# A 90-degree rotation of 96 planes: the first store waits for the loads, and the group of four slabs goes fourth

## The chip, the core and the metric

The kernel runs on one core of one Trainium2 chip. The metric is the device time in microseconds (us). Before the change it is 123.41 us, the median of three runs (123.36 to 123.59).

## The reference

The input `x` has 32 x 3 planes of 256 x 256 float32 numbers, 25.17 MB. Each plane is turned by 90 degrees clockwise; nothing is calculated.

```python
def reference(x):
    return np.rot90(x, k=-1, axes=(-2, -1)).astype(np.float32)
```

Every byte must be read once and written once, so 50.33 MB pass through the DMA engines.

## The kernel before

**Tiling.** The input is seen as 24,576 rows of 256 numbers and cut into 12 slabs of 2,048 rows (2 MB each): a slab is 128 partitions x 16 rows, 16 KB in each partition. All 12 slabs fit on the chip at once. They are held in five groups, given by `sizes` (line 38): 2, 2, 4, 2, 2 slabs. Each group has one tile `u0` to `u4` (line 41), and nothing in it is used twice: data come in, are turned in place, and go out from the same tile. Small side buffers hold what an in-place turn would overwrite: `spare[0]` and `spare[1]` in PSUM (line 45) and `extra` in SBUF (line 46), each half a slab.

**Loads.** SyncE (SP) issues all DMAs. Group 0 comes in with three transfers (lines 55 and 56: 1, 1 and 2 MB). Each later group comes in with as many transfers as it has slabs, 2 MB each (line 61). A transfer takes every I-th partition (`[i::I]`, with I the slabs of the group) and two runs `a` in each. That makes 13 loads. Loads have no wait of their own except that the program has eight semaphores for landings, used in turn: a transfer's issue waits until the transfer eight places ahead has landed.

**Turning.** VectorE (DVE) does the turning by 32 x 32 transposes of a quarter of two slabs at a time, 128 x 2048 numbers in one instruction, four for a group of two slabs and eight for the group of four. For groups 1 to 4 (`turn_group`, lines 77 to 95) it first transposes one quarter per pair of slabs into a side buffer (line 85), then the other three in place (line 90); then ScalarE (ACT) copies the held quarter back (line 95). Group 0 has its own form (lines 65 to 75). Line 97 says which side buffer a group uses: group 1 `extra`, group 2 both spares, group 3 `spare[0]`, group 4 `spare[1]`.

**Stores.** After all of that, in program order, stand the stores, 2 MB each: two for group 0 (line 103), then for each group two per pair of slabs (line 108), each from every second partition (`[a::2]`). That makes 12 stores. They stand behind the loads in SP's order, and each waits for its data, for its landing semaphore and for nothing else. All 25 transfers go through one hardware queue. Descriptors move 8, 16 or 32 KB at a time.

The program's order of the groups is the order of loading, of turning and of storing.

Of the kernel before, what the change touches and what calls it, by code (L numbers as in the profile page):

```python
# [1 line left out]

# [4 lines left out]


@with_exitstack  # L10
def kernel(
    ctx: ExitStack,
    tc: tile.TileContext,
    x: bass.AP,
    out: bass.AP,
):

    nc = tc.nc
    fp32 = mybir.dt.float32

    B, C, H, W = x.shape
    P = nc.NUM_PARTITIONS
    R = 16  # L30
    E = R * W
    hw = R // 2
    low, high = slice(0, hw), slice(hw, R)

    rows_in = x.rearrange("b c h w -> (b c h) w")
    rows_out = out.rearrange("b c h w -> (b c h) w")

    sizes = (2, 2, 4, 2, 2)
    first = [sum(sizes[:n]) for n in range(len(sizes))]
    groups = [  # L40
        ctx.enter_context(tc.tile_pool(name=f"group{n}", bufs=1)).tile([P, s, E], fp32, name=f"u{n}")
        for n, s in enumerate(sizes)
    ]
    psum = ctx.enter_context(tc.tile_pool(name="psum", bufs=1, space=bass.MemoryType.PSUM))
    spare = [psum.tile([P, E // 2], fp32, name=f"spare{h}") for h in range(2)]
    extra = ctx.enter_context(tc.tile_pool(name="extra", bufs=1)).tile([P, E // 2], fp32, name="extra")

    def rows_of(rows, n):
        return rows[first[n] * P * R : (first[n] + sizes[n]) * P * R]


    ld = rows_of(rows_in, 0).rearrange("(s i p r) w -> s i p (r w)", s=2, i=2, p=P)
    home = [groups[0][:, s].rearrange("p (i f) -> p i f", i=2) for s in range(2)]
    for i in range(2):
        nc.sync.dma_start(out=home[0][:, i], in_=ld[1, i])  # L55
    nc.sync.dma_start(out=home[1], in_=ld[0].transpose([1, 0, 2]))  # L56
    for n in range(1, len(sizes)):
        I = sizes[n]
        ld = rows_of(rows_in, n).rearrange("(a i m r) w -> i m a (r w)", a=2, i=I, m=P // I)
        for i in range(I):  # L60
            nc.sync.dma_start(  # L61
                out=groups[n].rearrange("p s f -> p (s f)").rearrange("p (a f) -> p a f", a=2)[i::I],
                in_=ld[i])

    def turn_slab(src, dsts):
        s = src.rearrange("p (i r g c) -> p c r g i", i=2, r=R // 2, c=R)
        for h, d in enumerate(dsts):
            d = d.rearrange("p (c k r) -> p c r k", c=hw, r=R // 2)[:, :, ::-1, ::-1]
            nc.vector.transpose(out=d, in_=s[:, h * hw : (h + 1) * hw])  # L69

    u = groups[0]
    turn_slab(u[:, 0], spare)
    turn_slab(u[:, 1], [u[:, 0, : E // 2], u[:, 0, E // 2 :]])
    for h in range(2):
        nc.scalar.copy(out=u[:, 1, h * E // 2 : (h + 1) * E // 2], in_=spare[h])  # L75

    def turn_group(n, held):
        I = sizes[n]
        T = I // 2
        K = W // (R * T)  # L80
        u = groups[n].rearrange("p s f -> p (s f)")
        src = u.rearrange("p (a t r g c) -> p t c r g a", a=2, t=T, r=R, c=R)
        dst = u.rearrange("p (i c k t r) -> p t c r k i", i=I, c=R, k=K, t=T)[:, ::-1, :, ::-1, ::-1, :]
        for t in range(T):
            nc.vector.transpose(  # L85
                out=held[t].rearrange("p (i c k r) -> p c r k i", i=I, c=hw, k=K)[:, :, ::-1, ::-1, :],
                in_=src[:, t, low, low])
        for c, r in ((low, high), (high, high), (high, low)):
            for t in range(T):
                nc.vector.transpose(out=dst[:, t, c, r], in_=src[:, t, c, r])  # L90
        back = u.rearrange("p (i c k t r) -> p t i c k r", i=I, c=R, k=K, t=T)[:, ::-1]
        for t in range(T):
            kept = held[t].rearrange("p (i c k r) -> p i c k r", i=I, c=hw, k=K)
            for i in range(I):
                nc.scalar.copy(out=back[:, t, i, low, :, high], in_=kept[:, i])  # L95

    for n, held in enumerate(([extra], spare, [spare[0]], [spare[1]]), 1):
        turn_group(n, held)


    st = rows_of(rows_out, 0).rearrange("(s i m r) w -> i m s (r w)", s=2, i=2, m=P // 2)
    for a in range(2):
        nc.sync.dma_start(out=st[a], in_=groups[0][a::2])
    for n in range(1, len(sizes)):
        st = rows_of(rows_out, n).rearrange("(a i m r) w -> a m i (r w)", a=2, i=sizes[n], m=P // 2)
        for i in range(0, sizes[n], 2):
            for a in range(2):
                nc.sync.dma_start(out=st[a][:, i : i + 2], in_=groups[n][a::2, i : i + 2])


# [1 line left out]
_INS = ['x']  # L112
_OUTS = [((32, 3, 256, 256), 'float32')]


# [23 lines left out]
```

## Time and profile before

| | us |
|---|---|
| Median of three runs | 123.41 |
| The profiled execution's own time | 123.44 |
| Its span, from the first to the last instruction | 121.6 |
| DVE busy, 24 instructions | 87.4 |
| ACT busy, 17 instructions | 14.9 |
| First transfer issued / first packet moves | 0.73 / 1.74 |
| Last of the 13 loads landed | 62.44 |
| Last of the 12 stores landed | 120.79 |

The span is the part that the trace covers; 1.8 us of the execution's time lie around it. A transfer has three times in the trace: when its instruction was issued on SP, when its packets moved on each of the 16 DMA engines, and when each engine's completion reached the semaphore; it has landed when the last of the 16 has. Rows that are marked SPq are SP's sequencer issuing DMAs. "a <- b" in the waits says that a stood idle until b was done.

### The profile page before, as it was taken

The page shows a single profiled execution, that of the slowest core. Times are in us where ns is not written, and L with a number is a line of the kernel's source. Part 1 is how long each engine was busy: PE and PEld are TensorE (multiplying, and loading weights), DVE is VectorE, ACT ScalarE, POOL GpSimd, SP SyncE. Part 2 cuts the span into 40 slices and gives each one's busy share as a digit, 9 for nine tenths or more (in the row PEclk, how much of TensorE's full clock was granted, in tenths as well). Part 3 has the DMA queues.
Part 4 walks back from the last instruction along what each step waited for, and adds up shares of the span by engine and source line. Part 5 has one row for each costly group of instructions (what it writes and reads, how often), then busy time and mean ns, then how long its engine had stood idle before and what let it go on. Part 6 is the DMA issues. An engine that isn't in the chain of part 4 may idle for free.

```text
span 121.6 us, 130 instructions
## 1 busy us (share of the span) xinstructions
DVE 87.4 (72%) x24; ACT 14.9 (12%) x17; POOL 0.2 (0%) x4
## 2 busy tenths in 40 slices
DVE  0039999999994099999999949999999995000000
ACT  0000400470004100000000354000240004100000
POOL 0000000000000000000000000000000000000000
DMA  4999999998989899999999999999999999999993
GB/s 92 423 426 434 442 431 431 436 506 356 506 356 506 350 431 431 426 431 431 377 409 431 431 431 431 442 431 431 431 431 442 431 436 431 431 431 431 431 431 135
DMA packets 3472, 50.33 MB, mean 414 GB/s; under 512 B 400, under 2 KB 400, under 8 KB 400
## 3 DMA queue, kind: packets, MB, share of 16 engines
q1 hardware_dynamic: 3472, 50.33, 97.7%
HBM read 25.17 MB, written 25.17 MB: 414 GB/s over the span
## 4 chain that ended last, share of the span: by engine, by line
DVE 42%; DMA 30%; issue 7%; SPq 4%; ACT 2%; ACTq 1%; DVEq 0%
DVE u L90 30%; DMA u<-in_x_dram 30%; DVE spare L85 12%; SPq L61 3%; ACT u L95 2%; ACTq L134 1%; SPq L55 1%; SPq L56 0%; DVEq L85 0%
## 5 line engine op out<-in xcount | busy, mean ns | idle before, releaser
L90 DVE STREAM_TRANSPOSE u<-u 128x2048 f32<-128x2048 f32 x15 | 54.7, 3665 | 0.4
L85 DVE STREAM_TRANSPOSE spare<-u 128x2048 f32<-128x2048 f32 x4 | 14.3, 3586 | 5.9 <-DMA u<-in_x_dram 4.3
L95 ACT COPY u<-spare 128x512 f32<-128x512 f32 (+1 forms) x12 | 8.0, 743 | 55.9 <-DVE u L90 55.9
L69 DVE STREAM_TRANSPOSE spare<-u 128x2048 f32<-128x2048 f32 x2 | 7.1, 3584 | 8.1 <-DMA u<-in_x_dram 8.1
L69 DVE STREAM_TRANSPOSE u<-u 128x2048 f32<-128x2048 f32 x2 | 7.8, 3990 | 0.0
L75 ACT COPY u<-spare 128x2048 f32<-128x2048 f32 x2 | 3.6, 1870 | 8.7 <-DVE u L69 8.7
L85 DVE STREAM_TRANSPOSE extra<-u 128x2048 f32<-128x2048 f32 x1 | 3.9, 3899 | 0.0
L95 ACT COPY u<-extra 128x1024 f32<-128x1024 f32 x2 | 2.0, 1043 | 11.3 <-DVE u L90 11.3
L75 ACT ACT_TABLE_LOAD x1 | 1.3, 1283 | 13.1 <-DMA u<-in_x_dram 13.1
L123 POOL MEMSET const-bfloat16-1.0<- 128x1 bf16 x1 | 0.1, 101 | 0.0
L123 POOL MEMSET const-uint8-127<- 128x1 uint8 x1 | 0.1, 101 | 0.0
L123 POOL MEMSET const-float32-0.0<- 128x1 f32 x1 | 0.1, 98 | 0.2 <-issue 0.2
L123 POOL MEMSET const-float32-1.0<- 128x1 f32 x1 | 0.1, 98 | 0.0
## 6 DMA issues: line engine op xcount, KB each, us to landing
out_dram<-u SPq DMA_DIRECT2D x12, 2048.0 KB, 20.6
u<-in_x_dram SPq DMA_DIRECT2D x11, 2048.0 KB, 32.3
u<-in_x_dram SPq DMA_DIRECT2D x2, 1024.0 KB, 5.8
```

Of the source, the lines that this page charges most:

```text
L55: nc.sync.dma_start(out=home[0][:, i], in_=ld[1, i])
L61: nc.sync.dma_start(out=groups[n].rearrange("p s f -> p (s f)").rearrange("p (a f) -> p a f", a=2)[i::I], in_=ld[i])
L69: nc.vector.transpose(out=d, in_=s[:, h * hw : (h + 1) * hw])
L75: nc.scalar.copy(out=u[:, 1, h * E // 2 : (h + 1) * E // 2], in_=spare[h])
L85: nc.vector.transpose(out=held[t].rearrange("p (i c k r) -> p c r k i", i=I, c=hw, k=K)[:, :, ::-1, ::-1, :], in_=src[:, t, low, low])
L90: nc.vector.transpose(out=dst[:, t, c, r], in_=src[:, t, c, r])
L95: nc.scalar.copy(out=back[:, t, i, low, :, high], in_=kept[:, i])
L123: nc = _bacc.Bacc("TRN2", target_bir_lowering=False, num_devices=1)
L134: with _tile.TileContext(nc) as tc:
```

## The change

The groups are now 2, 2, 2, 4, 2 slabs: the group of four is loaded, turned and stored fourth, not third. The side buffers follow: group 1 `extra`, group 2 `spare[1]`, group 3 both spares, group 4 `extra`. The last load of 2 MB is cut into two of 1 MB, the first of which is called `mark`. The first store gets a dependency on `mark`, so that it waits until that load has landed, when 1 MB of loads is still to come. The stores of a group are two transfers whatever its size, so that the group of four leaves in two of 4 MB in place of four of 2 MB. There are now 14 loads and 10 stores.

```diff
-    sizes = (2, 2, 4, 2, 2)
+    sizes = (2, 2, 2, 4, 2)
...
     for n in range(1, len(sizes)):
         I = sizes[n]
         ld = rows_of(rows_in, n).rearrange("(a i m r) w -> i m a (r w)", a=2, i=I, m=P // I)
+        to = groups[n].rearrange("p s f -> p (s f)").rearrange("p (a f) -> p a f", a=2)
         for i in range(I):
-            nc.sync.dma_start(
-                out=groups[n].rearrange("p s f -> p (s f)").rearrange("p (a f) -> p a f", a=2)[i::I],
-                in_=ld[i])
+            if (n, i) == (len(sizes) - 1, I - 1):
+                mark = nc.sync.dma_start(out=to[i::I, 0], in_=ld[i][:, 0])
+                nc.sync.dma_start(out=to[i::I, 1], in_=ld[i][:, 1])
+            else:
+                nc.sync.dma_start(out=to[i::I], in_=ld[i])
...
-    for n, held in enumerate(([extra], spare, [spare[0]], [spare[1]]), 1):
+    for n, held in enumerate(([extra], [spare[1]], spare, [extra]), 1):
         turn_group(n, held)
...
     for a in range(2):
-        nc.sync.dma_start(out=st[a], in_=groups[0][a::2])
+        put = nc.sync.dma_start(out=st[a], in_=groups[0][a::2])
+        if a == 0:
+            tc.add_manual_dep(put.ins, mark.ins.name, mybir.DependencyInfo(
+                mybir.DependencyClass.Sync, mybir.DependencyReason.SCHED_ONLY), reason="stores after loads")
     for n in range(1, len(sizes)):
         st = rows_of(rows_out, n).rearrange("(a i m r) w -> a m i (r w)", a=2, i=sizes[n], m=P // 2)
-        for i in range(0, sizes[n], 2):
-            for a in range(2):
-                nc.sync.dma_start(out=st[a][:, i : i + 2], in_=groups[n][a::2, i : i + 2])
+        for a in range(2):
+            nc.sync.dma_start(out=st[a], in_=groups[n][a::2])
```

## The prediction

> **What bounds the kernel now.** I read the page first, its busy shares and its slices.
>
> ```profile
> DVE 87.4 (72%) x24; ACT 14.9 (12%) x17; POOL 0.2 (0%) x4
> ...
> DMA  4999999998989899999999999999999999999993
> GB/s 92 423 426 434 442 431 431 436 506 356 506 356 506 350 431 431 426 431 431 377 409 431 431 431 431 442 431 431 431 431 442 431 436 431 431 431 431 431 431 135
> ...
> q1 hardware_dynamic: 3472, 50.33, 97.7%
> ```
>
> DVE, the busiest engine, works 87.4 us of 121.6; the DMA engines are taken for 97.7%. The rate is near 431 GB/s whether they load (left half) or store (right half); the 506/356 pattern is 32 KB packets counted where they start. So the DMA queue is the bound, and only its idle or slow stretches can be won. Second, the stretches:
>
> ```profile
> 0.00:1.70 1.70, 0.00 (x0) 0.00 (x0) 0.20 (x4) 1.00 0.00 0
> 1.70:59.00 57.30, 46.39 (x13) 6.91 (x5) 0.00 (x0) 1.00 1.01 425
> 59.00:62.00 3.00, 3.00 (x2) 0.00 (x0) 0.00 (x0) 1.00 0.96 339
> 62.00:119.60 57.60, 38.06 (x11) 7.96 (x12) 0.00 (x0) 1.00 1.01 431
> 119.60:121.60 2.00, 0.00 (x0) 0.00 (x0) 0.00 (x0) 1.00 0.16 66
> ```
>
> The last two columns are DMA share and GB/s. Besides the head (1.7 us) and the tail, one place is slow: 59 to 62 us, where the queue passes from loads to stores. At 431 GB/s its bytes would take 3.00 x 339 / 431 = 2.36 us, so 0.64 us is lost. The landing records say the same: loads of 2 MB with 16 KB packets land 4.89 us apart (the 10th at 47.10, 11th 52.00, 12th 56.89), the last takes 5.55 (62.44), and stores then land every 4.84 to 4.89 us. The loss is 5.55 - 4.89 = 0.66 us on the slowest DMA engine. The 16 completions of one transfer, 0.43 us apart until then, are 0.82 us apart from there to the end: half of the engines lost some 0.25 us, half 0.6. Packets that otherwise take 0.61 us take 0.7 to 1.27 from about 59.1 us on, two microseconds before the last load's packets end.
>
> Third, SP's waits, which say why stores are already queued at that time:
>
> ```profile
> SPq L108 <- DVE u L90: 52.6, 4, 28.5
> SPq L61 <- DMA u<-in_x_dram: 14.7, 4, 4.3
> SPq L103 <- DMA u<-in_x_dram: 8.3, 2, 4.2
> ```
>
> A transfer is issued when the one eight places ahead has landed, so the first stores (the 14th and 15th transfers) go out at 27.73 and 32.51, as loads 6 and 7 land, and two of group 1 at 40.06 and 42.22. They lie behind the last loads in one queue, which keeps its order: nothing is stored until the loads are through.
>
> **The change, part by part.**
>
> *The group of four goes fourth.* The same bytes are loaded: 32 KB packets (steps of 4.855 us) and 16 KB packets (4.89) change places, sum unchanged. New landings from these steps: group 2 at 32.6, group 3 at 52.0, group 4 last. DVE goes through group 0 as now (8.1 to 23.1) and group 1 (to 38.0), then group 2 at once: 3.6 + 10.9 (a group of two with its side buffer in PSUM, the timeline's rows from 72.94 to 87.51) = 14.5, to 52.6, ACT's copies to 54.5. Group 3 takes 7.1 + 21.9 = 29.0, to 81.6; its second transpose needs `spare[1]` and comes at 56.2, after ACT's copies. ACT then needs 3.1 more: 84.6. Group 4 takes 3.9 + 11.2 = 15.1 (group 1's rows), to 96.7, with copies 98.7. DVE's waits of 4.28 us (for the four slabs) and 1.63 us (for ACT) go, but what DVE gains is hidden: the queue has six 2 MB stores to do from about 61.8, to 61.8 + 6 x 4.863 = 91.0, so group 3 (84.6) comes 6.4 us early, and group 4 (98.7) is 12 us ahead of the queue's 110.4. Cost: 0. Should that cover fail, the queue would idle by whatever DVE is late; it would take 6.4 us.
>
> *The cut load and the joined stores.* 25 transfers become 24. A transfer's completion takes each engine one packet of 9 ns and a gap, about 13 ns; two 1 MB loads at the start landed 2.51 us apart, half of the next 2 MB's 4.97. So: -0.01 us. Joined stores keep 16 KB packets; their steps should be 9.7 us. A 4 MB issue on SP is not in the trace: a 2 MB one takes 0.60 to 1.35 us, so between 0.60 and 2 x 1.35 = 2.7; the queue holds over 4 us of work then, so 0 either way.
>
> The Trainium skill ("DMA: Bandwidth & Descriptors", section Bandwidth) gives transfers of 1 MB 78% of the peak; by it the two halves would cost 0.6 us more each. The two 1 MB loads in this queue show no such loss, so I leave it out.
>
> *The wait of the first store.* Behind it on SP stand only the nine other stores and the end; no engine waits for a store. What matters is whether the DMA engines run dry before its packets come. `mark` would land at 56.89 + 4 packets x 0.613 + 0.01 = 59.36 on the slowest engine, if nothing slows it. An issue follows a landing by 0.02 to 0.09 us (42.21 to 42.22; 27.64 to 27.73): 59.45. From issue to first packet, the one place with an idle queue is the program's start: issue 0.73, packet 1.74, so 1.01 us: 60.46. A store's issue takes 0.60 to 0.65 against that one's 0.37; if packets come only after it ends, 60.74. Without the slow stretch, load packets end at 61.0 on the fastest engine, 61.43 on the slowest (12th transfer's completion packets at 56.1 to 56.4, plus 4.9). So the store's packets arrive 0.3 to 1.0 us before an engine is dry. Not free is the ramp: the first 8 KB packet took 1.1 us, later ones 0.31, so 0.8 us of ramp from HBM; for a read from SBUF there is no row, between 0 and that. With all 0.8 the first store packet ends at 60.46 + 0.8 + 0.61 = 61.87, or 62.15 from 60.74; without any delay the slowest engine would end it at 61.43 + 0.61 = 62.04. So the late arrival costs 0 to 0.11 us.
>
> What it may win are the 0.66 us. I take them to come from stores standing ready behind the loads: the engines begin reading for stores while load data are still arriving, as the slow packets fit that begin 2 us before the loads end. Held, the stores arrive when at most one packet per engine is left. Bounds: nothing is won (the loss belongs to the change of direction), or all of it, 0.66. I take nearly all, since the slow packets are load packets, which no stores would stand beside before 60.46.
>
> The skill's rule against it is in the same page, section Rules for kernel authors: issue a DMA early and wait late, so that its fixed cost is hidden. Its first-byte time for queues of this kind (some 0.6 us, section Latency and other measured facts) would put the first store packets at 60.05, earlier than the row's 1.01 us does; the row is used.
>
> **Sum**, against the profiled execution (123.44; the median of the runs is 0.03 less): last load lands at 56.89 + 4.90 = 61.79, not 62.44; the stores take 58.35 - 0.03 as now; last landing 120.11 against 120.79, so -0.68; ramp +0 to +0.11. That is 122.76 to 122.87: **122.8**.
>
> **Rivals.**
>
> *The loss stays.* Turning the queue from reading HBM to writing it costs 0.66 us wherever the stores come from. For it: stores land in an even step afterwards and the loss is a single one; against: it falls on loads. Time: 123.4 less 0.03. The same number results if the dependency turns out only to order the program and the store is issued as load 7 lands, at 32.6 us.
>
> *Slower: the engines need a longer lead than they get.* The slow packets begin 2 us before the loads end, so the engines may read about that far ahead. Held stores leave the reading side without work from about 59.1 to 60.46 or 60.74: 1.36 to 1.64 us. If that lead is lost, it decides as soon as the lead needed exceeds the 0.3 to 1.0 us left. Price: where the turn's own loss stays too, up to 1.64 us, to 125.0; where some of it is covered by packets in flight, half, 0.7 us: 124.1. For it: 1.1 us for the first packet at the start. Against: that ramp was HBM's, and a stored packet is read from SBUF.
>
> **Numbers.** Held and the loss gone (122.7 to 123.1): 0.52. Loss stays or is not held (123.2 to 123.6): 0.27. Engines run dry (123.7 to 125): 0.21. The range goes from 122.5 (the bound 122.76 less 0.2 for run-to-run spread, as the three runs differ by 0.23) to 124.1, which leaves out half of the last case. 0.2%, 0.25 us, is about what a measurement of this kernel can tell from no change: faster 0.52, same 0.27, slower 0.21. The likeliest case's own range is 122.6 to 123.1.
>
> **What would show it.** The first store issued near 59.4 us and not 27.7; `mark` landed just before, the last load at 61.8; the GB/s in 59 to 62 near 425; the spread of 16 completions staying near 0.43 us; last landing near 120.1, span near 121.0. DVE ends near 96.7 with no wait over 1 us after 23 us. If the last load lands at 61.8 but the first store over 5.2 us later, the engines ran dry. If it lands at 62.4 again, the turn itself costs. The prediction is wrong in kind if group 3's stores are issued after 91.

## The result and the profile after

The changed kernel takes 122.94 us (median of six runs, 122.88 to 123.17), the kernel before, beside it, 123.58 us (123.36 to 123.62): a ratio of 0.996 (95% interval 0.9946 to 0.9973). Between the medians that is 0.64 us less, between the means 0.54. In a later series the same pair gave 123.03 against 123.36, 0.33 us less, ratio 0.9975 (0.9965 to 0.9984). The profiled execution of the changed kernel took 122.88 us, with a span of 121.09 us (before: 123.44 and 121.65).

First the page of the changed kernel, its busy times and slices:

```profile
DVE 87.4 (72%) x24; ACT 14.9 (12%) x17; POOL 0.2 (0%) x4
...
DMA  2999999999989898999999999999999999999994
GB/s 89 428 428 422 452 433 433 433 433 433 520 346 520 346 520 346 428 422 411 433 433 428 433 433 428 417 417 433 428 433 433 433 433 433 433 433 433 433 422 184
...
q1 hardware_dynamic: 3456, 50.33, 97.6%
```

DVE works as long as before. The dip in the middle of the GB/s row (377 and 409 before, at slices 20 and 21) is gone; the 520/346 pattern, the four-slab group's 32 KB packets, has moved to the right. The stretches of the changed kernel, with the same columns as those shown of before:

```profile
0.00:1.70 1.70, 0.00 (x0) 0.00 (x0) 0.20 (x4) 1.00 0.00 0
1.70:59.00 57.30, 50.69 (x14) 8.84 (x7) 0.00 (x0) 1.00 1.00 425
59.00:62.00 3.00, 2.97 (x2) 0.00 (x0) 0.00 (x0) 1.00 1.03 437
62.00:119.60 57.60, 33.71 (x10) 6.10 (x10) 0.00 (x0) 1.00 1.00 428
119.60:121.10 1.50, 0.00 (x0) 0.00 (x0) 0.00 (x0) 1.00 0.01 0
```

The third row is the gain: 437 GB/s from 59 to 62 us where 339 stood. The fourth has a small part of it given back: 428 against 431. When the stores were issued, from the timeline of SP in the changed kernel:

```profile
59.43 1.37 SPq L106 DMA_DIRECT2D out_dram<-u  x2
60.92 25.39 SPq L113 DMA_DIRECT2D out_dram<-u  x6
```

And what SP waited for there (total us, times, longest):

```profile
SPq L106 <- DMA u<-in_x_dram: 31.2, 1, 31.2
SPq L113 <- DVE u L93: 24.3, 2, 14.7
```

The first store stands 31.2 us at its wait for the load `mark` and goes out at 59.43; before, it went out at 27.73. The landing records show what came of it (last of the 16 completions of a transfer, in us):

| | before | after |
|---|---|---|
| 22 of 24 MB loaded | 56.89 | 56.82 |
| `mark` | | 59.29 |
| Last load | 62.44 | 61.74 |
| Last store | 120.79 | 120.28 |
| From last load to last store | 58.35 | 58.54 |
| Spread of the 16 completions, last load | 0.82 | 0.28 |

The last 2 MB took 4.92 us and not 5.55: 0.63 us won at the turn. Of it, 0.19 us is lost again on the way to the end, so that the last store lands 0.51 us earlier. DVE's one wait for a load in the changed kernel is the first, until 8.06 us, and it no longer waits for ACT; its last transpose ends at 95.9.

### The profile page after: what moved, and what is told of

Same layout as the page of the kernel before. It is cut to its first block, busy times and chain, and to the rows that moved or that the text cites. A ratio compares the mean times of both kernels' runs of the same rounds, so it can differ in the third digit from the quotient of the medians.

```text
span 121.1 us, 131 instructions
## 1 busy us (share of the span) xinstructions
DVE 87.4 (72%) x24; ACT 14.9 (12%) x17; POOL 0.2 (0%) x4
## 4 chain that ended last, share of the span: by engine, by line
DVE 66%; issue 6%; DMA 6%; ACT 1%; ACTq 1%; SPq 0%; DVEq 0%
DVE u L93 39%; DVE spare L88 9%; DVE extra L88 6%; DVE u L72 6%; DVE spare L72 6%; DMA u<-in_x_dram 6%; ACT u L98 1%; ACTq L139 1%; SPq L55 0%; DVEq L88 0%; DVEq L72 0%
## 5 line engine op out<-in xcount | busy, mean ns | idle before, releaser
L72 DVE STREAM_TRANSPOSE spare<-u 128x2048 f32<-128x2048 f32 x2 | 7.1, 3586 | 8.1 <-DMA u<-in_x_dram 8.1
L98 ACT COPY u<-spare 128x512 f32<-128x512 f32 (+1 forms) x10 | 6.0, 687 | 38.5 <-DVE u L93 38.5
L88 DVE STREAM_TRANSPOSE spare<-u 128x2048 f32<-128x2048 f32 x3 | 10.7, 3588 | 0.0
L88 DVE STREAM_TRANSPOSE extra<-u 128x2048 f32<-128x2048 f32 x2 | 7.8, 3896 | 0.0
L98 ACT COPY u<-extra 128x1024 f32<-128x1024 f32 x4 | 4.0, 1043 | 22.8 <-DVE u L93 22.8
```

The lines of the kernel that those rows point to most:

```text
L88: nc.vector.transpose(out=held[t].rearrange("p (i c k r) -> p c r k i", i=I, c=hw, k=K)[:, :, ::-1, ::-1, :], in_=src[:, t, low, low])
```

## The experiments

Two theories at first. **H**: stores that stand ready behind the last loads cost 0.66 us at the turn, and the hold saves it. **G**: the gain comes from the new order of the groups or the joined stores. The prediction's slower rival, that the engines need a longer lead of store packets than 1 MB gives, is tested beside them. The lead is the time from the moment when the first store's packets could start to the end of the load packets. Each run was timed beside the kernel before on its own chip; that kernel's medians were 123.34 to 123.54 us there, its single runs 123.04 to 123.93. Of each kernel's runs a single one, the profiled execution, has a trace. Of each edit the lines that matter are shown, with ... for others, against the changed kernel unless said otherwise.

### The hold alone, and the rest alone

The kernel before with the cut load and the held store (its order and its 2 MB stores kept), shown against the kernel before:

```diff
+            if (n, i) == (len(sizes) - 1, I - 1):
+                mark = nc.sync.dma_start(out=to[i::I, 0], in_=ld[i][:, 0])
+                nc.sync.dma_start(out=to[i::I, 1], in_=ld[i][:, 1])
...
+            tc.add_manual_dep(put.ins, mark.ins.name, mybir.DependencyInfo(
...
```

> The order of the groups (2, 2, 4, 2, 2) and the 2 MB stores of the kernel before; only the cut last load and the held first store are taken from the change. Theory H (stores standing ready behind the last loads cost 0.66 us, and holding them back saves it): the last two loads land 2.45 us apart, the last near 61.8 us, the 16 completions stay about 0.3 to 0.4 us apart, and the time is 122.9 us (122.75 to 123.1). Theory G (the gain is the new order or the joined stores): the last load lands near 62.4 and the time is 123.4 to 123.6. Third possibility: less than 122.75, if the joined 4 MB stores of the change cost something.

Measured: 123.25 us, ratio 0.9989 (0.9977 to 1.0). The time lies between the two theories' ranges. The turn itself went as H says: the last load landed at 61.84, 4.90 us after the load of 22 MB, and the row of its stretches is as in the changed kernel:

```profile
59.00:62.00 3.00, 3.00 (x2) 0.00 (x0) 0.00 (x0) 1.00 1.03 437
```

The changed kernel without hold and cut:

```diff
-                mark = nc.sync.dma_start(out=to[i::I, 0], in_=ld[i][:, 0])
-                nc.sync.dma_start(out=to[i::I, 1], in_=ld[i][:, 1])
+                nc.sync.dma_start(out=to[i::I], in_=ld[i])
...
-        put = nc.sync.dma_start(out=st[a], in_=groups[0][a::2])
-        if a == 0:
-            tc.add_manual_dep(put.ins, mark.ins.name, mybir.DependencyInfo(
...
+        nc.sync.dma_start(out=st[a], in_=groups[0][a::2])
```

> The order 2, 2, 2, 4, 2 and the joined stores of the change, with the last load whole and no store held. Theory H: the first store is issued at about 32 us, the step to the last load is 5.4 to 5.6 us and not 4.9, DVE ends near 97 us as in the changed kernel, and the time is 123.4 to 123.7 us. Theory G: the step is 4.9 us and the time 122.9.

Measured: 123.47 us, ratio 1.0008 (0.9995 to 1.0021). The last load came 5.79 us after the one before, at 62.68:

```profile
59.00:62.00 3.00, 2.97 (x2) 0.00 (x0) 0.00 (x0) 1.00 0.93 295
```

So the hold, with the cut load, repairs the turn, and the new order and the joined stores don't: for the turn G falls. That the cut alone does it is excluded by a run further below, in which the last load is whole, all stores are held, and the load is on time. But of the 0.84 us between the two last loads (62.68 and 61.84) only 0.22 us is left between the medians. In the traces 0.64 us is left between the last stores (120.37 and 121.01): 0.2 us goes in the stores, which is the second question. The rest is a difference between executions. The traced ones lie at opposite ends of their kernels' runs, 123.08 us with the hold (second fastest of 12) and 123.67 us without it (second slowest of 12), and no trace explains that spread.

### How much of the loads must be left

The hold moved to the load before, with the last load whole, so that 2 MB are left:

```diff
+            put = nc.sync.dma_start(out=to[i::I], in_=ld[i])
+            if (n, i) == (len(sizes) - 1, I - 2):
+                mark = put
...
```

> The changed kernel with the last load whole, and the first store held until the load before it has landed, so that 2 MB of loads are still to come. The first store is issued at 56.9 us and its packets may start at 57.9 to 58.2; the slow packets in the kernel before began at 59.1. Theory H with a reach of some 2 us ahead (engines begin reading for a store when it is near enough): the loss is back in full, last load 5.4 to 5.6 us after the one before, time 123.4 to 123.7. Theory S (only stores that have long stood in the queue, or several of them, cost): no loss, 122.9.

Measured: 123.24 us, ratio 0.9988 (0.9975 to 1.0). The first store was issued at 57.10; the last load landed 5.45 us after the one before, nearly as late as without any hold:

```profile
59.00:62.00 3.00, 2.97 (x2) 0.00 (x0) 0.00 (x0) 1.00 1.03 377
```

At the turn this is theory H; the time is in neither theory's range, and no longer than with the hold alone (123.25), although the last load came 0.57 us later. The traced execution, 123.41 us, is the second slowest of 12. Whether the turn is as late in the faster ones isn't shown.

Next, the hold on the last load itself:

```diff
+            put = nc.sync.dma_start(out=to[i::I], in_=ld[i])
+            if (n, i) == (len(sizes) - 1, I - 1):
+                mark = put
...
```

> The changed kernel with the last load whole, and the first store held until all loads have landed. The last load lands at 61.75 us, the first store is issued at 61.8, its first packet starts 1.0 us later (62.8; 63.1 if it comes only after the issue). The load packets end at 61.1 to 61.4, so the engines stand dry for 1.4 to 2.0 us. Theory H: that idle time and the ramp of a first store packet (0 to 0.8 us beyond its 0.61) are the whole price: 1.4 to 2.5 us over the changed kernel, 124.3 to 125.4 us, and the trace gives the ramp. Rival of the prediction (engines need a longer lead than 1 MB gives): the price is less, under 1 us, since the changed kernel would have paid most of it already: under 123.9.

It did something else. Of group 0's two stores only one was held, and the other was put ahead of it and issued at 27.89 us, so that 2 MB stood ready for 33 us; the held one went out at 62.55. Measured: 123.32 us, ratio 0.9996 (0.9984 to 1.0009), last load 5.53 us after the one before. One ready store of 2 MB is thus enough for the whole loss. With a dependency on the whole last load for all ten stores:

> The changed kernel with the last load whole, and every store held until all loads have landed (in the run that was to do this, one store of 2 MB still went out at 27.9 us, as only the other was held). The last load lands at 61.75 us without the loss; the first store is issued at 61.8 and its packets start at 62.8 to 63.1, when the engines have been dry for 1.4 to 2.0 us. Theory H: the price is that idle time and a ramp of 0 to 0.8 us, so 1.4 to 2.5 us over the changed kernel of this call. Rival of the prediction (a longer lead is needed than 1 MB gives): under 1 us over it.

Measured: 125.49 us, ratio 1.0175 (1.0161 to 1.0189), 2.46 us over the changed kernel's 123.03 beside it. The last load landed 4.89 us after the one before, on time, and it is whole: it is the hold that repairs the turn, not the cut. Its stretches around the turn and SP's first stores:

```profile
59.00:62.00 3.00, 2.97 (x2) 0.00 (x0) 0.00 (x0) 1.00 0.62 262
62.00:65.00 3.00, 3.00 (x2) 0.00 (x0) 0.00 (x0) 1.00 0.63 262
```

```profile
62.08 1.32 SPq L104 DMA_DIRECT2D out_dram<-u  x2
```

The DMA share, next to last, is 0.62 and 0.63 in the two stretches: the engines were dry on both sides of 62 us, for 1.9 to 2.4 us each. In the packet records the last load packets end at 61.1 to 61.4, and the first store packets start at 63.38 to 63.53, 1.30 to 1.45 us after the issue. They take 612 to 621 ns, so there is next to no ramp: what costs is the issue. With 0.5 MB left, all stores held by the same dependency (shown is the cut of the load):

```diff
-                nc.sync.dma_start(out=to[i::I, 1], in_=ld[i][:, 1])
+                mark = nc.sync.dma_start(out=to[i::I, 1, : E // 2], in_=ld[i][:, 1, : E // 2])
+                nc.sync.dma_start(out=to[i::I, 1, E // 2 :], in_=ld[i][:, 1, E // 2 :])
...
```

> The changed kernel with the last 1 MB cut again, and all stores held until 0.5 MB of loads is still to come. The mark lands near 60.5 us, the first store is issued at 60.6, its packets can start at 61.6 to 61.9, and the load packets end at 61.0 to 61.4: the engines stand dry for 0.2 to 0.9 us. Theory H: the time is 0.2 to 1.2 us over the changed kernel of this call, with stores that land late by as much. Rival of the prediction: the same as the changed kernel, since both would come too late for the lead.

Measured: 124.32 us, ratio 1.0081 (1.0068 to 1.0095), 1.29 us over the changed kernel, just above H's range. The first store was issued at 60.67, its packets started from 61.99 to 62.15, and the engines were dry for 0.7 to 1.1 us:

```profile
59.00:62.00 3.00, 2.97 (x2) 0.00 (x0) 0.00 (x0) 1.00 0.66 276
```

The price follows the dry time, not a lead beyond it: with 1 MB left the packets can start at 59.43 + 1.30 = 60.73, the load packets end at 61.0 to 61.3, and the changed kernel's lead is thus some 0.3 to 0.5 us. The slower rival falls as it was put. Then 1.5 MB, cut as 0.5, 0.5 and 1 MB:

```diff
-                mark = nc.sync.dma_start(out=to[i::I, 0], in_=ld[i][:, 0])
+                mark = nc.sync.dma_start(out=to[i::I, 0, : E // 2], in_=ld[i][:, 0, : E // 2])
+                nc.sync.dma_start(out=to[i::I, 0, E // 2 :], in_=ld[i][:, 0, E // 2 :])
```

> The changed kernel with the last 2 MB loaded as 0.5, 0.5 and 1 MB and the first store held until the first of these has landed: 1.5 MB of loads is still to come. The mark lands near 58.1 us, the first store is issued at 58.2, and its packets can start 1.3 us later (measured where the queue was dry), at 59.5, while load packets end at 61.0 to 61.3. With 1 MB left that lead is 0.2 to 0.5 us and nothing is lost; with 2 MB it is some 2.7 us and 0.55 us is lost. Theory H with a fixed reach of two microseconds: the lead of 1.5 to 1.8 us is inside it, so part of the loss is back: the last load lands 0.2 to 0.6 us late, time 123.1 to 123.5. Theory of a count (a loss as soon as stores can be read beside loads, at whatever lead): the same full loss of 0.55. If the last load is not late: the loss needs more than 1.8 us of lead, and the time is that of the changed kernel.

Measured: 122.82 us against 123.54, ratio 0.995 (0.9933 to 0.9967), the largest gain of all by its middle value, though its interval overlaps the changed kernel's and the two were not timed side by side. The first store was issued at 58.29, a lead of 1.4 to 1.8 us, and the last load landed on time at 61.84:

```profile
59.00:62.00 3.00, 2.96 (x2) 0.00 (x0) 0.00 (x0) 1.00 1.03 437
```

So the loss sets in between a lead of 1.8 us (none) and of some 2.6 us (2 MB left: 57.10 + 1.30 = 58.40 against 61.0; 0.55 us). The reach of two microseconds, with part of the loss at 1.5 MB, was wrong, and so was the theory of a count. SP's issuing isn't the cause either: here SP issues four stores from 58.29 to 62.0 us and the load is on time, while in the kernel before it issues nothing from 42.8 to 74.4 us and the load is late. A finer test of the reading ahead was a store cut so that one packet for each engine (0.25 MB) stands ready:

```diff
+        parts = ((slice(0, 16), 0), (slice(0, 16), 1), (slice(16, 64), slice(0, 2))) if a == 0 else ((slice(0, 64), slice(0, 2)),)
...
```

> The changed kernel with the first store cut so that 0.25 MB of it (16 partitions, one packet of 16 KB for each DMA engine) is not held and stands in the queue behind the loads from about 28 us on; all other stores are held until 1 MB of loads is left. With 2 MB standing ready the loss was full (5.53 us to the last load for 4.89). If the engines read ahead for stores by as many packets as stand ready, one packet each: the last load lands 0.1 to 0.3 us late. If any ready store is enough, since what costs is that the two directions overlap at all: 0.5 to 0.65 us late. If one packet is too little: on time, 4.90 us after the load two before it.

Measured: the piece was issued at 32.73 us and the last load landed on time (4.89 us after 22 MB), so one ready packet costs nothing at the turn. But the time was 124.99 us, ratio 1.0123 (1.0102 to 1.0143), lost in the stores behind it:

```profile
62.00:65.00 3.00, 3.00 (x2) 0.00 (x0) 0.00 (x0) 1.00 1.00 366
65.00:68.00 3.00, 2.96 (x2) 0.00 (x0) 0.00 (x0) 1.00 1.00 344
```

After the cut store the 16 completions are 2.4 us apart, packets take up to 2.0 us between 62 and 68 us, and three stores took 2.2 to 2.3 us each to issue. That comes with the pieces of 16 and 48 partitions; why stays open.

### What takes part of it back

The changed kernel again beside the others, and with 2 MB stores for the group of four:

> The changed kernel once more, beside the other three, since the hold alone came to 0.9989 of the kernel before (0.9977 to 1.0) and the change itself to 0.996. Theory H (the hold is all of the gain): the ratio lies with that of the hold alone, between 0.996 and 0.999. Theory H+G (the new order or the joined stores add some 0.3 us, which the hold alone lacks): 0.995 to 0.997.

```diff
-        for a in range(2):
-            nc.sync.dma_start(out=st[a], in_=groups[n][a::2])
+        for i in range(0, sizes[n], 2):
+            for a in range(2):
+                nc.sync.dma_start(out=st[a][:, i : i + 2], in_=groups[n][a::2, i : i + 2])
```

> The changed kernel with the group of four stored in four transfers of 2 MB and not in two of 4 MB. In the changed kernel the stores took 58.54 us from the last load's landing to the last store's, against 58.35 before, and their packets rose from 611 to about 615 ns after 84 us, as the 4 MB stores were issued. If the joined stores do that: 58.35 us and 0.2 us less than the changed kernel. If they don't: the same time within 0.1 us, and packets of 615 ns again, as the hold alone showed with 2 MB stores.

Measured: 123.03 us, ratio 0.9975 (0.9965 to 0.9984), for the changed kernel; 123.21 us, ratio 0.999 (0.9981 to 0.9998), with 2 MB stores, where packets also rise to 617 ns (the two intervals just overlap). The first lies in H's range, by which the hold is all of the gain, and yet the joined stores are worth 0.18 us here, more than half of what the change gives beside them (0.33), and not by the way expected: they don't raise the packets' time. How they do it isn't shown; in the traces only 0.09 us of it stands between last load and last store (58.63 for 58.54). The new order of the groups gives nothing that these runs can tell: the hold alone had 0.9989 with the old order, this has 0.999 with the new. Mean times of a 16 KB store packet, from the packet records, show where the time goes:

| kernel | lead of the first store, us | ns to 84 us | 84 to 90 | 100 to 119 | last load to last store, us |
|---|---|---|---|---|---|
| before | stands ready | 611.0 | 611.0 | 611.0 | 58.35 |
| 2 MB left | 2.6 to 3.1 | 611.0 | 611.0 | 611.0 | 58.34 |
| 1.5 MB left | 1.4 to 1.8 | 611.0 | 611.1 | 611.0 | 58.23 |
| changed (1 MB left) | 0.3 to 0.5 | 612.0 | 617.8 | 615.8 | 58.54 |
| 0.5 MB left | dry 0.7 to 1.1 | 617.8 | 621.4 | 615.7 | 59.73 |
| all loads landed | dry 1.9 to 2.4 | 618.4 | 621.6 | 615.7 | 60.96 |

The 4 MB stores are issued from 84.2 to 86.3 us. A first theory, P, was that engines that start their packets together hinder each other, since the loss at the turn had spread them (0.82 to 1.05 us) and the hold had not. To spread them without it, 16 pieces of 7 KB were loaded behind the last 1 MB, all into one unused buffer:

```diff
+    for k in range(0, 16, 8):
+        nc.sync.dma_start(out=junk[k : k + 8], in_=rows_in[k * 7 : (k + 8) * 7].rearrange("(p r) w -> p (r w)", p=8))
```

> The changed kernel with 16 pieces of 7 KB loaded in addition, behind the last 1 MB, into a buffer that nothing reads, each time 8 partitions; eight of the 16 DMA engines should carry them, so that these start to store 0.5 us after the others. It is to tell why the store packets take about 615 ns in the kernels that hold the stores and 611 in those that don't. Theory P (engines that start their packets together hinder each other; the loss at the turn spreads them, 16 completions 0.82 to 1.05 us apart, the held stores leave them 0.25 to 0.35 apart): completions 0.8 to 0.9 us apart, packets of 611 ns with no spread, stores of 4.86 us, so that of the 0.55 us which the pieces cost some 0.2 to 0.3 come back: 0.25 to 0.4 us over the changed kernel, 123.2 to 123.5. Without P: packets of 615 ns in spite of the spread, and 0.5 us over it.

Measured: 123.93 us, ratio 1.004 (1.0025 to 1.0055), more than either theory gave. The pieces disturbed the turn themselves (store packets beside them took up to 1.09 us, and the 16 completions were 1.4 us apart, not 0.8 to 0.9), and then packets took 611 ns until 84 us and 613 to 614 after. By itself this settles nothing; but the run with 1.5 MB left, timed beside it, has completions only 0.37 us apart and packets of 611.0 to the end, so P falls.

What fits all rows is theory **R**: the lead at the turn is a reserve of store packets that lasts; where it is small, each disturbance, such as the issue of a new store, uses some of it, and from then on packets take 615. The times agree: in the changed kernel the mean rises to 618 to 622 ns from 84 to 88 us and to 619 to 620 from 98 to 102, just as two stores each are issued (84.25 to 86.3 and 97.94 to 99.98), and it is 613 to 616 between and behind; with 1.5 MB left the same issues leave it at 611. The test of R is the kernel before with the hold at 1.5 MB and nothing else:

> The kernel before (its order 2, 2, 4, 2, 2 and its 2 MB stores) with the first store held until 1.5 MB of loads is left. Theory R (the lead that store packets have over the end of the loads is a reserve that lasts to the end; with 1 MB left it is 0.2 to 0.5 us and is used up, and then packets take 615 ns; with 1.5 MB left it is 1.4 to 1.8 us and packets stay at 611; order and joined stores matter only where there is no reserve): last load near 61.85, store packets 611 ns to the end, 2 MB stores 4.86 us apart, 0.6 to 0.75 us less than the kernel before. Theory J (the joined 4 MB stores, not the lead, kept the packets at 611 with 1.5 MB left): packets rise to 615 after the stores issued at 74 us, as with the hold of 1 MB alone, and the time is 0.1 to 0.3 us below the kernel before.

Measured: packets 611.1 ns in every stretch, 2 MB stores 4.83 to 4.90 us apart, 58.25 us from last load to last store. The last load landed 4.92 us after the load of 22 MB, on time:

```profile
59.00:62.00 3.00, 3.00 (x2) 0.00 (x0) 0.00 (x0) 1.00 0.99 421
```

The packets do as R says, and J falls. That the lead decides the packets' time is thus shown in both orders; the reserve itself stands in no trace and stays R's picture of it. The time is 123.03 against 123.43 us, ratio 0.9968 (0.9956 to 0.998): 0.40 us less, not the 0.6 to 0.75 of R. In its profiled execution the loads themselves ended 0.17 us later than in the run with 1.5 MB left and the new order (62.01 against 61.84), all of it already there at the fourth load (18.08 against 17.89), long before the hold acts.

## Why the prediction was right

It gave 122.8 us and 0.6 us less than before; measured were 122.94 and 0.64, 122.88 and 0.56 in the profiled executions. That the two differences agree so closely is in part luck: beside the change the kernel before took 123.58 and not 123.41, and in the later series the gain was 0.33. By its steps:

- **The bound.** The DMA queue, right: DVE lost its waits of 4.28 and 1.63 us and was done 6 us earlier, and yet the new order and the joined stores without the hold took 1.0008 of the time before.
- **The group of four.** Group 3's first store was forecast for 84.6 and issued at 84.25, group 4's for 98.7 and at 97.94. Cost 0, as forecast.
- **Cut load and joined stores.** `mark` and the last load landed 2.45 us apart, so cutting costs nothing. The joining was taken as nothing. With the hold it is worth 0.18 us, a term that the sum lacks; without the hold nothing can be seen.
- **The loss at the turn.** Forecast for the last load 61.79, measured 61.74. "All of it, 0.66" was right: 0.63. Its cause, stores standing ready while loads are still arriving, is borne out by ten profiles: the last load was late by 0.55 to 0.9 us in the four kernels where 2 MB or more of stores stood ready 2.6 us or longer before the loads' end, and on time in the six runs that held them to 1 or 1.5 MB. That the loss belongs to the change of direction is refuted for these traces, as the held turns have no such loss on either side. What is not shown is that each run of a kernel pays it in full: the medians of the hold alone and of the run with 2 MB left are equal. That the engines "read ahead some 2 us" stays an inference: a lead of 1.8 us costs nothing and one of 2.6 us nearly all, which a simple reach doesn't explain.
- **The late packets.** 59.45 was forecast for the issue, 59.43 measured, which is luck: `mark` landed 0.07 us earlier than forecast, and the issue followed it by 0.14 us, not 0.02 to 0.09. Of the two values for the first packets the later one, 60.74, was right if the 1.30 us of the runs with a dry queue hold here too; in the changed kernel itself this can't be seen. The ramp of up to 0.8 us isn't there. The end of the loads on the slowest engine, 61.43, doesn't follow from the figures beside it (56.43 + 4.90 = 61.33; measured 61.26), so the bound of 0.11 us should have been 0.2; without a ramp it doesn't matter.
- **The step that was mis-sized**: "the stores take 58.35 - 0.03 as now". They took 58.54, 0.22 us more, and so the last store landed at 120.28 and not at 120.11. In these stores packets take 612 to 618 ns in the mean and not 611, with a lead of 0.3 to 0.5 us; with 1.4 to 1.8 us they took 611 and the stores 58.23 to 58.25.
- **The slower rival** named the right quantity, the lead, and the wrong threshold: 1 MB is enough not to run dry, and too little to keep the packets at 611 ns.

What stays open: how ready stores slow the last loads, why packets stay at 615 ns after a turn with a small lead, how the joined stores gain 0.18 us, and why the kernel before differs by up to 0.9 us between its own runs. That spread is larger than the gain, and a difference between two traces is worth no more than the medians allow.

## What to carry to other kernels

Where one queue passes from loads to stores, look at the step between landings there: stores that stand ready behind the loads cost this kernel 0.55 to 0.9 us, stores that come too late cost all the time the engines are dry, and between them lay a window. Size the hold from the trace. Here some 0.47 us pass from a load's last packet to its landing, 0.14 us to the issue and 1.30 us to the first packet, 1.9 us in all. At 431 GB/s 1.5 MB last 3.65 us, which leaves a lead of some 1.75 us; with 1 MB (2.43 us) the lead is some 0.5 us, the turn is as good, and part of it is given back in the stores. When a repaired stall shows less in the total than in its own place, compare the packets' mean time on both sides of it, and look where the traced execution lies among the kernel's runs.

## What the runs showed of the hardware

A first store on a dry queue had its first packet 1.30 to 1.48 us after its issue began (0.65 to 0.67 us of which is the issue), a first load at the program's start 1.01 us (issue 0.37). Store packets of 16 KB took 611.0 to 611.1 ns in the mean over 58 us where the first store had a lead of 1.4 us or more. With a lead of 0.3 to 0.5 us or none it was 612 to 622 ns, although in the changed kernel no engine was idle (16 packets were under way at all times from 64 to 118 us). A 4 MB store takes no longer to issue than a 2 MB one: 0.60 us for the first of a pair and 1.41 for the second, as for the 2 MB pair behind it (0.60 and 1.40).
